# First normalization set by set beside the modulation weights, and the position table as a row part and a column part

## Chip, cores and metric

The kernel runs on one core of a Trainium2 chip. The metric is the device time in microseconds of one execution of the whole program. A profile is one more execution, recorded instruction by instruction; its span runs from the first instruction to the last.

## The reference

One inference step of a network with two layers over 512 latent tokens (a grid of 8 rows and 64 columns) and 128 context tokens, 1024 channels, everything in fp32. Cut to what matters here:

```python
xc, xl = x_prompt, x_sample + grid_pos_embed(512, 1024)   # channels: sin/cos of the row, sin/cos of the column
for l in range(2):
    mod = silu(c) @ w_mod[l] + b_mod[l]                   # for context and for latent tokens: 3 * 1024 values
    shift, scale, gate = split(mod, 3)
    h = rmsnorm(x, norm_g[l]) * (1 + scale) + shift
    z = h @ w_in[l]                                       # inputs of three mixers, their gates, the merge gates
    y_hy = hyena(z...) * silu(gate); y_s5 = s5(z...) * ...; y_gdn = deltanet(z...) * ...
    x = x + gate * (merge(y_hy, y_s5, y_gdn) @ w_out[l])
```

The first half of the position channels (sin and cos of the row) depends on the token's row alone, the second half on its column alone.

## The kernel before

Activations lie transposed: channels on the 128 partitions, in 8 channel tiles (KT = 8), and 640 tokens along each partition. A matrix product in fp32 is made of three matmuls of halves (`mm3`): an operand is split into a rounded part and its remainder (`split`: a cast on ScalarE at L69, a subtraction at L70 on VectorE or, for the gates' weights, on GpSimd). A projection tile is 48 such matmuls (L91), in two weight pieces of 4 channel tiles each; `wr` is a raw weight piece, `wh` and `wl` are its parts, `hh` and `hl` those of the normalized input. Tiles named `pj` are projections of the mixers, tiles named `pg` are gates, which depend on `hh` and `hl` alone and serve as filling work.

`start` does what comes ahead of layer 0: SP loads x (five pieces `xi`), the position table (`pos`) and four sets of modulation weights (`wm`, 2048 KB each); TensorE transposes x channel tile by channel tile (L129), VectorE adds `pos` (L271), ScalarE squares and VectorE sums the squares (L320 to L324), and `rstd_cols` makes 1/rms of each token (`rstd`, L338). `mod_set` multiplies one weight set (L286), copies the result out of PSUM (`mrow`, L289), transposes it and adds the biases (`mod`, L136, L138). Set s gives shift and scale of the channel tiles s and 4 + s alone. `norm_h` spreads `rstd` over the partitions (`dg` L136, two matmuls with ones L352 and L353, copy to `rs` L354) and then normalizes the 8 channel tiles: multiply on VectorE (`xn`), two activations on ScalarE (`hf`, L362), `split` to `hh` and `hl`.

After it the hyena and S5 stage runs, two generators taken in turn, with the gates 0 to 13 as filling work. The S5 tables begin with two powers on GpSimd (`stp` L698 from the step sizes `in_ls`, `smag` L703); the S5 transposes L129 of `M` and products L908 need these tables. The last matmuls of a hyena block are its synthesis (L468 to L473). Then comes the DeltaNet stage with the other gates, then the merge, and the same again for layer 1.

The code is not run in the order in which it is written: a scheduling pass with a timeline of its own places every instruction on its engine's queue, and each queue then runs strictly in that order. A tile in reused memory waits for the tile that it replaces.

Of the kernel before, what the change touches and what calls it, by code (L numbers as in the profile page):

```python
# [12 lines left out]
F32 = mybir.dt.float32  # L13
F32R = mybir.dt.float32r
AF = mybir.ActivationFunctionType
ALU = mybir.AluOpType
# [36 lines left out]
def bc(ap, shape):  # L53
    return ap.to_broadcast(shape)


class Net:
# [98 lines left out]
    def run(self):  # L156
        tc, nc, a = self.tc, self.nc, self.a
        with ExitStack() as es:
# [9 lines left out]
            with self.pool(name="pm0", bufs=4, space=PSUM) as self.pm:  # L168
                self.start()
            for l in range(self.depth):  # L170
                with self.pool(name="pmn", bufs=2, space=PSUM) as self.pm:
                    self.norm_h(l)
# [58 lines left out]
    def start(self):  # L231
# [20 lines left out]
        with self.pool(name="st", bufs=2) as p:  # L252
# [3 lines left out]
            pos = [p.tile([128, KT // 2, NLAT], F32, name="pos%d" % h, bufs=1) for h in range(2)]  # L256
            for h in range(2):
                nc.sync.dma_start(pos[h], a["pos"][4 * h:4 * h + 4].rearrange("k p t -> p k t"))
# [5 lines left out]
            for k in range(KT):  # L264
# [6 lines left out]
                nc.vector.tensor_tensor(xk[:, :NLAT], ps, pos[k // 4][:, k % 4, :], op=ALU.add)  # L271
                nc.scalar.copy(xk[:, NLAT:], pc[:, :128])
                self.square_acc(p, k, xk)
                nc.sync.dma_start(self.xd[0][k], xk)
                self.xs.append(xk)
            for s in range(4):
                self.mod_set(0, s, [wm[s][:, k] for k in range(KT)], self.bank(), self.bank(), p)

# [61 lines left out]
    def norm_h(self, l):  # L340
# [3 lines left out]
        md = self.mod[l]  # L344
        with self.pool(name="nm", bufs=2) as p:
            r = self.rstd
            dg = p.tile([128, 5, 128], F32, name="dg", bufs=1)
            for t in range(5):
                self.ts(nc.vector, dg[:, t, :], self.ident, r[:, t:t + 1])
            rs = p.tile([128, NTOK], F32, name="rs", bufs=1)  # L350
            pa, pb = self.bank(), self.bank()
            nc.tensor.matmul(pa, self.ones, dg[:, 0:4, :], start=True, stop=True)  # L352
            nc.tensor.matmul(pb[:, :128], self.ones, dg[:, 4, :], start=True, stop=True)  # L353
            nc.scalar.copy(rs[:, :NLAT], pa)  # L354
            nc.vector.tensor_copy(rs[:, NLAT:], pb[:, :128])
            for k in range(KT):
                xk = self.xs[k]
                t = p.tile([128, NTOK], F32, name="xn")
# [1190 lines left out]
def _f(x):  # L1549
    return np.ascontiguousarray(x, dtype=np.float32)  # L1550
# [148 lines left out]
```

## Time and profile before

| | before |
|---|---|
| median of 3 runs (lowest to highest) | 3738.56 us (3723.69 to 3741.91) |
| profiled execution | 3732.11 us |
| its span | 3730.3 us |
| mean granted TensorE clock | 0.95 |
| busy: TensorE matmuls / VectorE / ScalarE / GpSimd | 91% / 64% / 38% / 52% |

The busy shares are means over stages with different limits. The profiled execution is one of its own, and times inside it are set against its own time.

### The profile page before, as it was taken

To read this page: it belongs to the slowest core of one execution; us is meant where nothing else is said; L and a number is where in the kernel's file an instruction comes from. 1 tells how busy PE (TensorE), PEld (TensorE's weight loads), DVE (VectorE), ACT (ScalarE), POOL (GpSimd) and SP (SyncE) were. 2 spreads that over 40 slices of the span, in tenths; PEclk is the share of its full clock that TensorE was granted. 3 is DMA by queue.
4 is the path that set the end of the run, shared out by engine and by line. 5 is a ranking of instruction groups with operands and counts; after the bars stand their busy time and mean duration, and the time that the engine had idled before them with its cause. 6 is when DMAs were issued, how large, how long until landed. Compare 5 with 4: busy or idle time off the path is not lost. (4 is left out here: it accounts for less than half of the span.)

```text
span 3730.3 us, 68509 instructions
## 1 busy us (share of the span) xinstructions
PE 3380.0 (91%) x25850; PEld 3220.4 (86%) x25850; DVE 2369.6 (64%) x4615; ACT 1413.4 (38%) x3295; POOL 1942.9 (52%) x2153
## 2 busy tenths in 40 slices
PE   6899898999979898899979999999989898898998
PEld 5798878888979887799978889988889898797998
DVE  6777677777227873743747776677773378875354
ACT  4433232332244445443334333323322545445422
POOL 4777777776345443401336777878763544341010
PEclk7999899999989998999989999999999999899999
DMA  6322334322232212533633222233222322134352
GB/s 242 110 73 82 94 107 115 108 73 63 78 93 65 68 62 68 170 126 109 188 113 98 75 71 83 81 75 81 76 66 77 92 64 78 41 97 139 125 178 89
DMA packets 310602, 363.05 MB, mean 97 GB/s; under 512 B 86814, under 2 KB 190270, under 8 KB 310016
## 3 DMA queue, kind: packets, MB, share of 16 engines
q1 hardware_dynamic: 305368, 358.01, 32.6%
q8 instruction: 204, 3.34, 0.4%
q10 hardware_dynamic: 4904, 0.66, 0.1%
q14 instruction: 126, 1.03, 0.1%
HBM read 291.87 MB, written 66.67 MB: 96 GB/s over the span
## 5 line engine op out<-in xcount | busy, mean ns | idle before, releaser
L91 PE MATMUL pj<-hh,wh 128*128 128x320 f32 x2048 | 666.4, 326 | 60.5 <-ACT wh L69 32.2
L91 PE MATMUL pj<-hh,wl 128*128 128x320 f32 x2048 | 655.5, 322 | 10.5 <-DVE wl L70 8.0
L91 PE MATMUL pj<-hl,wh 128*128 128x320 f32 x2048 | 657.9, 321 | 5.5 <-DVE hl L70 5.4
L70 POOL TENSOR_TENSOR wl<-wr,wh 128x512 fp32r<-128x512 f32 x288 | 392.1, 1365 | 448.9 <-ACT wh L69 388.7
L69 ACT CAST wh<-wr 128x512 fp32r<-128x512 f32 x608 | 374.8, 618 | 659.7 <-PE pj L91 486.3
L91 PEld LDWEIGHTS pj<-hh,wh 128*128 128x128 f32 x2048 | 400.7, 196 | 70.8 <-ACT wh L69 33.6
L91 PE MATMUL pg<-hh,wh 128*128 128x320 f32 x1280 | 415.1, 325 | 15.2 <-ACT wh L69 10.5
L91 PE MATMUL pg<-hh,wl 128*128 128x320 f32 x1280 | 407.6, 323 | 9.3 <-POOL wl L70 9.2
L70 DVE TENSOR_TENSOR wl<-wr,wh 128x512 fp32r<-128x512 f32 x320 | 259.5, 812 | 244.4 <-ACT wh L69 243.1
L91 PEld LDWEIGHTS pj<-hh,wl 128*128 128x128 f32 x2048 | 398.8, 195 | 14.9 <-DVE wl L70 9.3
L91 PE MATMUL pg<-hl,wh 128*128 128x320 f32 x1280 | 411.5, 322 | 0.0
L91 PEld LDWEIGHTS pj<-hl,wh 128*128 128x128 f32 x2048 | 400.3, 195 | 11.1 <-DVE hl L70 8.8
L91 PE MATMUL pj<-yh,wh 128*128 128x320 f32 x1024 | 318.0, 312 | 6.5 <-ACT yh L69 5.1
L91 PE MATMUL pj<-yl,wh 128*128 128x320 f32 x1024 | 318.9, 312 | 2.6 <-DVE yl L70 2.5
L91 PE MATMUL pj<-yh,wl 128*128 128x320 f32 x1024 | 317.5, 311 | 0.0
L91 PEld LDWEIGHTS pg<-hh,wh 128*128 128x128 f32 x1280 | 250.4, 196 | 19.4 <-ACT wh L69 11.6
L91 PEld LDWEIGHTS pg<-hh,wl 128*128 128x128 f32 x1280 | 247.4, 194 | 14.2 <-POOL wl L70 12.5
L91 PEld LDWEIGHTS pg<-hl,wh 128*128 128x128 f32 x1280 | 249.5, 195 | 0.9 <-issue 0.4
L91 PEld LDWEIGHTS pj<-yh,wh 128*128 128x128 f32 x1024 | 193.4, 189 | 8.1 <-ACT yh L69 5.9
L91 PEld LDWEIGHTS pj<-yl,wh 128*128 128x128 f32 x1024 | 193.5, 189 | 4.8 <-DVE yl L70 4.8
L91 PEld LDWEIGHTS pj<-yh,wl 128*128 128x128 f32 x1024 | 193.6, 189 | 0.0
L1514 POOL TENSOR_TENSOR m<-m,gt 128x640 f32<-128x640 f32 x16 | 31.1, 1943 | 295.8 <-DVE gt L132 295.8
(523 smaller groups left out, 8673.3 us busy)
## 6 DMA issues: line engine op xcount, KB each, us to landing
wr<-in_wt SPq DMA_DIRECT2D x608, 256.0 KB, 2.7
gt<-gst SPq DMA_DIRECT2D x160, 160.0 KB, 2.0
gt<-gt SPq DMA_DIRECT2D x64, 320.0 KB, 3.4
wr<-in_wmod SPq DMA_DIRECT2D x64, 256.0 KB, 3.3
Pm<-gcd SPq DMA_DIRECT2D x32, 320.0 KB, 11.0
wm<-in_wmod SPq DMA_DIRECT2D x4, 2048.0 KB, 16.8
M<-ks SPq DMA_DIRECT2D x256, 32.0 KB, 1.8
us<-u SPq DMA_DIRECT2D x16, 328.0 KB, 4.2
```

What stands on the lines that cost most here:

```text
L69: self.nc.scalar.copy(h, src)
L70: (eng or self.nc.vector).tensor_tensor(l, src, h.bitcast(F32), op=ALU.subtract)
L91: ins = self.nc.tensor.matmul(o, w[:, k, :m], x[:, kh * 4 + k, s], start=kh == 0 and k == 0 and i == 0, stop=kh == 1 and k == 3 and i == 2)
L1514: nc.gpsimd.tensor_tensor(m[i], m[i], g, op=ALU.add)
```

## The change

- The position table comes as 8 row values and 64 column values for each channel (128 x 288 numbers in place of two halves of 128 x 4 x 512), is loaded ahead of x, and the add at L271 repeats it along the grid.
- `norm_h` keeps the spreading of `rstd`; the normalization of one channel tile is `norm_k`. In layer 0 both are called in `start`: the spreading ahead of the weight sets, and after set s the tiles s and 4 + s. Layer 1 keeps its order.
- The PSUM pool of `start` has 6 buffers, not 4; the pool of the normalization is open during `start`; the stores of x (`xd`) are written behind the sets.
- Six small loads of the hyena stage (`alt`, `hcw`, `hcb`, `fw1`, `fw2`, `fb`) are issued by SP and no longer by ScalarE.

```diff
-            with self.pool(name="pm0", bufs=4, space=PSUM) as self.pm:
+            with self.pool(name="pm0", bufs=6, space=PSUM) as self.pm:
                 self.start()
             for l in range(self.depth):
-                with self.pool(name="pmn", bufs=2, space=PSUM) as self.pm:
-                    self.norm_h(l)
+                if l:
+                    with self.pool(name="pmn", bufs=2, space=PSUM) as self.pm, self.pool(name="nm", bufs=2) as p:
+                        self.norm_h(l, p)
+                        for k in range(KT):
+                            self.norm_k(l, k, p)
+                self.layer_dram(l)
...
-        with self.pool(name="st", bufs=2) as p:
+        with self.pool(name="nm", bufs=2) as pn, self.pool(name="st", bufs=2) as p:
+            pos = p.tile([128, 288], F32, name="pos", bufs=1)
+            nc.sync.dma_start(pos, a["pos"])
             xi = [p.tile([128, DM], F32, name="xi%d" % t, bufs=1) for t in range(5)]
             for t in range(5):
                 nc.sync.dma_start(xi[t], a["x"][t * 128:(t + 1) * 128])
-            pos = [p.tile([128, KT // 2, NLAT], F32, name="pos%d" % h, bufs=1) for h in range(2)]
-            for h in range(2):
-                nc.sync.dma_start(pos[h], a["pos"][4 * h:4 * h + 4].rearrange("k p t -> p k t"))
+
+            row = pos[:, 0:32].rearrange("p (k r) -> p k r", k=4)
+            col = pos[:, 32:288].rearrange("p (k c) -> p k c", k=4)
...
-                nc.vector.tensor_tensor(xk[:, :NLAT], ps, pos[k // 4][:, k % 4, :], op=ALU.add)
+                sh = [128, 8, 64]
+                g = bc(row[:, k, :].unsqueeze(2), sh) if k < 4 else bc(col[:, k - 4:k - 3, :], sh)
+                nc.vector.tensor_tensor(xk[:, :NLAT].rearrange("p (r c) -> p r c", r=8),
+                                        ps.rearrange("p (r c) -> p r c", r=8), g, op=ALU.add)
                 nc.scalar.copy(xk[:, NLAT:], pc[:, :128])
                 self.square_acc(p, k, xk)
-                nc.sync.dma_start(self.xd[0][k], xk)
                 self.xs.append(xk)
+            self.norm_h(0, pn)
             for s in range(4):
                 self.mod_set(0, s, [wm[s][:, k] for k in range(KT)], self.bank(), self.bank(), p)
+                for k in (s, 4 + s):
+                    self.norm_k(0, k, pn)
+            for k in range(KT):
+                nc.sync.dma_start(self.xd[0][k], self.xs[k])
...
-    def norm_h(self, l):
+    def norm_h(self, l, p):
...
+    def norm_k(self, l, k, p):
+
+        nc, md = self.nc, self.mod[l]
+        xk = self.xs[k]
+        t = p.tile([128, NTOK], F32, name="xn")
+        nc.vector.tensor_tensor(t, xk, self.rs, op=ALU.mult)
+        h = p.tile([128, NTOK], F32, name="hf")
+        for i, (s, e) in enumerate(((0, NLAT), (NLAT, NTOK))):
+            nc.scalar.activation(h[:, s:e], t[:, s:e], AF.Identity, bias=md[:, k, i:i + 1],
+                                 scale=md[:, 8 + k, i:i + 1])
+        self.split(self.hh[:, k, :], self.hl[:, k, :], h)
...
-            nc.scalar.dma_start(self.alt, a["alt"])
+            nc.sync.dma_start(self.alt, a["alt"])
             self.hcw = cp.tile([128, 24, 3], F32, name="hcw")
-            nc.scalar.dma_start(self.hcw, a["hcw"][l].rearrange("p (n c) -> p n c", n=24))
+            nc.sync.dma_start(self.hcw, a["hcw"][l].rearrange("p (n c) -> p n c", n=24))
             self.hcb = cp.tile([128, 24], F32, name="hcb")
-            nc.scalar.dma_start(self.hcb, a["hcb"][l])
+            nc.sync.dma_start(self.hcb, a["hcb"][l])
...
-            nc.scalar.dma_start(w1, a["fw1"][l])
+            nc.sync.dma_start(w1, a["fw1"][l])
             w2 = p.tile([64, 64], F32, name="w2")
-            nc.scalar.dma_start(w2, a["fw2"][l])
+            nc.sync.dma_start(w2, a["fw2"][l])
             fb = p.tile([64, 3], F32, name="fb")
-            nc.scalar.dma_start(fb, a["fb"][l])
+            nc.sync.dma_start(fb, a["fb"][l])
```

Since a scheduling pass sets the order, a few lines move many instructions. On ScalarE, from the weight sets to the first input projection, stood before (`mrow` is a set's copy out of PSUM, `lr`, `li`, `stp` are loads for the S5 tables):

```order
L323 ACTIVATE sqt<-x_219 128x640
L289 COPY mrow<-pb 128x128 x4
L692 DMA lr<-in_lr 128x64
L693 DMA li<-in_li 128x64
L695 DMA stp<-in_ls 64x64 x2
L354 COPY rs<-pb 128x512
L697 DMA s_542<-in_s 128x128
L784 DMA sd<-in_sd 128x16
L362 ACTIVATE hf<-xn,mod_91 128x512
L362 ACTIVATE hf<-xn,mod_91 128x128
L69 CAST wh<-wr 128x512 x2
```

and on the same engine stands now, for the second and third pair of channel tiles (`hh` is the cast that ends a tile's normalization on ScalarE):

```order
L69 CAST hh<-hf 128x640 x2
L302 COPY mrow<-pb 128x128
L377 ACTIVATE hf<-xn,mod_91 128x512
L377 ACTIVATE hf<-xn,mod_91 128x128
L377 ACTIVATE hf<-xn,mod_91 128x512
L377 ACTIVATE hf<-xn,mod_91 128x128
L69 CAST hh<-hf 128x640 x2
L302 COPY mrow<-pb 128x128
```

and behind that, for the fourth pair:

```order
L709 DMA lr<-in_lr 128x64
L710 DMA li<-in_li 128x64
L377 ACTIVATE hf<-xn,mod_91 128x512
L377 ACTIVATE hf<-xn,mod_91 128x128
L377 ACTIVATE hf<-xn,mod_91 128x512
L377 ACTIVATE hf<-xn,mod_91 128x128
L712 DMA stp<-in_ls 64x64 x2
L69 CAST hh<-hf 128x640
L714 DMA s_536<-in_s 128x128
L69 CAST hh<-hf 128x640
L801 DMA sd<-in_sd 128x16
L69 CAST wh<-wr 128x512 x6
```

The loads of `stp` stood ahead of all normalization and stand behind its last activations; the first weight casts (`wh`) stand behind its last cast; each set's copy stands behind the casts of the pair before.

On TensorE, the end of the sets before and their beginning now (`dg` times ones is the spreading of `rstd`, `sqs` the sum of squares):

```order
L129 MATMUL pb<-c_66,mrow 128x128
L286 MATMUL pb<-wm_120,csc 32x128 x32
L129 MATMUL pb<-c_66,mrow 128x128
L352 MATMUL pb<-dg,c_66 128x512
L353 MATMUL pb<-dg,c_66 128x128
L91 MATMUL pj<-hh,wh 128x320
```

and now:

```order
L346 MATMUL pb<-c_66,sqs 128x2 x5
L364 MATMUL pb<-dg,c_66 128x512
L365 MATMUL pb<-dg,c_66 128x128
L299 MATMUL pb<-wm_115,csc 32x128 x32
L129 MATMUL pb<-c_66,mrow 128x128
```

The spreading moved from behind the fourth set to ahead of the first.

On GpSimd, from the end of its constants, before and now (`wl` here are remainders of the gates' weights, `BR` the first product that needs the S5 tables):

```order
L843 MEMSET u 128x8x2
L698 TENSOR_TENSOR stp<-c_66,stp 128x64
L703 TENSOR_TENSOR smag<-c_66,smag 128x64
L70 TENSOR_TENSOR wl<-wr,wh 128x512 x2
L859 TENSOR_TENSOR BR<-lwr,sbr 128x128
```

and now:

```order
L860 MEMSET u 128x8x2
L715 TENSOR_TENSOR stp<-c_66,stp 128x64
L70 TENSOR_TENSOR wl<-wr,wh 128x512 x2
L720 TENSOR_TENSOR smag<-c_66,smag 128x64
L860 MEMSET u 128x8x2
L846 TENSOR_TENSOR E<-E 128x16
L70 TENSOR_TENSOR wl<-wr,wh 128x512 x2
L876 TENSOR_TENSOR BR<-lwr,sbr 128x128
```

Two weight remainders moved ahead of the second power, two more ahead of the first product.

Farther on, the rows of TensorE differ up to about 43% of their number, within the DeltaNet stage of layer 0, and are then the same but for a short stretch in the merge of layer 1. Ahead of the first S5 transposes of `M` stood 156 matmuls of L91 (48 `pj`, 28 `pg`, 48 `pj`, 32 `pg`); now 258. Between those transposes and the next groups stood 24, 12, 24, 23 of them. Ahead of the last synthesis of layer 0 stood 1028 of the layer's 2304 matmuls into `pg`; now 1271. In layer 1 it is 1425 in both.

## Rows read from the trace of the kernel before

**Rows 1.** Windows of the two layers: length, busy us (x instructions) by engine, granted clock, DMA.

```profile
100.00:989.00 889.00, 813.35 (x6322) 759.60 (x6322) 623.54 (x1003) 277.52 (x772) 648.78 (x760) 0.96 0.33 89
989.00:1908.00 919.00, 837.79 (x6489) 812.01 (x6488) 524.98 (x1273) 404.13 (x829) 302.58 (x298) 0.96 0.35 107
1958.00:2854.00 896.00, 835.02 (x6233) 794.81 (x6232) 626.05 (x950) 291.85 (x792) 665.35 (x758) 0.98 0.29 77
2854.00:3712.00 858.00, 792.21 (x6118) 767.31 (x6116) 497.34 (x1174) 379.06 (x777) 251.65 (x261) 0.94 0.32 99
```

**Rows 2.** Windows, the third 10 us, as in Rows 1; last column GB/s.

```profile
20.00:30.00 10.00, 4.45 (x53) 4.15 (x55) 5.27 (x8) 3.11 (x5) 1.73 (x4) 0.65 1.05 387
```

**Rows 3.** DMA view of the first 60 us: issues, KB each, us to landing.

```profile
pos<-in_pos SPq DMA_DIRECT2D x2, 1024.0 KB
```

**Rows 4.** Timeline, DMA issues on SP: start us, us, what.

```profile
24.29 5.20 SPq L487 DMA_DIRECT2D zt<-in_zt  x1
...
42.18 1.07 SPq L81 DMA_DIRECT2D wr<-in_wt  x2
```

**Rows 5.** Timeline, transposes to modulation: start us, us, engine, what [idle before].

```profile
13.99 2.67 DVE L271 TENSOR_TENSOR x<-pb,pos 128x512 f32<-128x512 f32 x4 [9.93 <-DMA pos<-in_pos]
...
20.99 4.53 DVE L324 TENSOR_TENSOR sqs<-sqs,sqt 128x640 f32<-128x640 f32 x5
...
28.21 1.17 POOL L338 TENSOR_TENSOR rstd<-rsv,c 128x5 f32<-128x5 f32 x1 [27.78 <-DVE rsv L138]
...
31.57 0.27 ACT L289 COPY mrow<-pb 128x128 f32<-128x128 f32 x1 [7.13 <-PE pb L286]
...
32.91 0.35 DVE L138 TENSOR_SCALAR mod<-mod,ng 128x2 f32<-128x2 f32 x2
...
40.04 3.58 PE L286 MATMUL pb<-wm,csc 128*32 128x128 f32 x64 [1.88 <-DMA wm<-in_wmod]
```

**Rows 6.** Timeline of VectorE: an add with a repeated operand.

```profile
107.45 0.67 DVE L894 TENSOR_TENSOR M<-T,BR 128x512 f32<-128x512 f32 x1
```

**Rows 7.** Timeline, first normalization and weight casts.

```profile
44.92 0.86 DVE L136 TENSOR_SCALAR dg<-c,rstd 128x128 f32<-128x128 f32 x4
...
47.38 0.58 ACT L354 COPY rs<-pb 128x512 f32<-128x512 f32 x1 [3.40 <-PE pb L353]
...
51.83 1.12 ACT L69 CAST wh<-wr 128x512 fp32r<-128x512 f32 x2
...
55.68 2.29 ACT L362 ACTIVATE hf<-xn,mod 128x512 f32<-128x512 f32 x4 [0.39 <-DVE hl L70]
...
57.87 1.34 ACT L69 CAST hh<-hf 128x640 fp32r<-128x640 f32 x2
```

**Rows 8.** Timeline of TensorE: first input projection, gates, first S5 transposes.

```profile
54.72 0.64 PE L91 MATMUL pj<-hh,wh 128*128 128x320 f32 x1 [7.36 <-ACT hh L69]
...
71.12 0.47 PE L91 MATMUL pj<-hh,wh 128*128 128x320 f32 x1
...
74.31 0.31 PE L91 MATMUL pg<-hh,wh 128*128 128x320 f32 x1
...
78.41 0.31 PE L91 MATMUL pj<-hh,wh 128*128 128x320 f32 x1
...
93.06 0.66 PE L129 MATMUL pb<-c,M 128*128 128x128 f32 x4 [0.80 <-DVE M L896]
...
116.11 0.39 PE L91 MATMUL pj<-hh,wl 128*128 128x320 f32 x1
```

**Rows 9.** Timeline, S5 step loads and GpSimd.

```profile
45.27 1.99 ACTq L695 DMA_DIRECT2D stp<-in_ls  x2
...
49.40 10.55 POOL L698 TENSOR_TENSOR stp<-c,stp 128x64 f32<-128x64 f32 x1 [17.09 <-DMA stp<-in_ls]
60.51 10.55 POOL L703 TENSOR_TENSOR smag<-c,smag 128x64 f32<-128x64 f32 x1 [0.56 <-DVE smag L701]
71.02 2.52 POOL L70 TENSOR_TENSOR wl<-wr,wh 128x512 fp32r<-128x512 f32 x2
```

More of the change, by code (lines that the diff above doesn't have):

```diff
@@ L343, in norm_h @@
         self.hl = self.hp.tile([128, KT, NTOK], F32R, name="hl", tag="hl")
[L344 to L358, printed above, removed]
-                nc.vector.tensor_tensor(t, xk, rs, op=ALU.mult)
-                h = p.tile([128, NTOK], F32, name="hf")
-                for i, (s, e) in enumerate(((0, NLAT), (NLAT, NTOK))):
-                    nc.scalar.activation(h[:, s:e], t[:, s:e], AF.Identity, bias=md[:, k, i:i + 1],
-                                         scale=md[:, 8 + k, i:i + 1])
-                self.split(self.hh[:, k, :], self.hl[:, k, :], h)
@@ new lines, in norm_h @@
+        r = self.rstd
+        dg = p.tile([128, 5, 128], F32, name="dg", bufs=1)
+        for t in range(5):
+            self.ts(nc.vector, dg[:, t, :], self.ident, r[:, t:t + 1])
+        self.rs = p.tile([128, NTOK], F32, name="rs", bufs=1)
+        pa, pb = self.bank(), self.bank()
+        nc.tensor.matmul(pa, self.ones, dg[:, 0:4, :], start=True, stop=True)
+        nc.tensor.matmul(pb[:, :128], self.ones, dg[:, 4, :], start=True, stop=True)
+        nc.scalar.copy(self.rs[:, :NLAT], pa)
@@ new lines, in norm_h @@
+        nc.vector.tensor_copy(self.rs[:, NLAT:], pb[:, :128])
+    def norm_k(self, l, k, p):
[8 more added lines that the diff above has]
+        self.split(self.hh[:, k, :], self.hl[:, k, :], h)
@@ L365, in norm_h, with layer_dram @@
+    def layer_dram(self, l):
         self.md = self.dp.tile([KT, 128, NTOK], F32, name="md%d" % l)
@@ L1569, in shape_constants @@
     pos = np.concatenate([np.sin(er), np.cos(er), np.sin(ec), np.cos(ec)], -1)
-    out["pos"] = _f(pos.T.reshape(KT, 128, NLAT))
+    pos = pos.T.reshape(KT, 128, NLAT)
+    out["pos"] = _f(np.concatenate([pos[0:4, :, ::64].transpose(1, 0, 2).reshape(128, -1),
+                                    pos[4:8, :, :64].transpose(1, 0, 2).reshape(128, -1)], 1))
     t = np.arange(256)[:, None] * 1.0
```

## The prediction, made before the changed kernel ran

> **What bounds the kernel now.** I read the page first (TensorE is the fullest engine and does the same work in both programs), then the windows of the stages, then the timeline of the first 120 us, engine by engine. In the windows the reader is to see that layer 0 and layer 1 spend their time alike and that TensorE is idle for little of it: 889 - 813.4 = 75.6 us and 919 - 837.8 = 81.2 us in layer 0, 61.0 and 65.8 us in layer 1 [rows 1]. No other engine is near that. So the kernel is TensorE's work plus its waits, and a lead that TensorE gains at the start is kept as far as later waits don't grow. In the timeline the start is a chain: position table and x in, transposes, squares, rstd, four sets of modulation weights, then the normalization of eight channel tiles on ScalarE and VectorE with TensorE trickling behind it; the first input projection begins at 54.72 and gives way to the gates only at 74.31 [rows 8].
>
> **The change part by part.**
>
> *Position table.* Two loads of 1024 KB go [rows 3]; 128 x 288 fp32 (144 KB) come. The 1904 KB less at 387 GB/s [rows 2] bring the weight sets in 5.0 us earlier. TensorE waits for a set only once, 1.88 us for the fourth [rows 5], so this alone is worth about 2 us. The first add waited for the table until 13.99 [rows 5]; now the transposes set its time. The five squares summed last, 4.53 us [rows 5], stay, so I take their end from 25.52 to 23.8 (bounds 25.5 and 22.5). The add with a repeated operand is not in the trace in this form: eight adds at 2.67 / 4 = 0.67 us [rows 5], and a VectorE operation with a repeated operand and as many elements takes 0.67 us too [rows 6], so no cost.
>
> *Rstd row ahead of the sets.* From the end of the squares to rstd it takes 29.38 - 25.52 = 3.86 us [rows 5], so rstd stands at 27.7. From the first diagonal tile to the end of the row's copy: 47.96 - 44.92 = 3.0 us [rows 7], so the row is there at 30.8. This step is now ahead of the first set on TensorE, which before started during rstd: set 0 runs 30.3 + 3.58 [rows 5] = 33.9. From a set's copy out of PSUM to its modulation columns: 33.26 - 31.57 = 1.7 us [rows 5], so the first pair of channel tiles can start at 35.6.
>
> *Pairs.* ScalarE needs 2.29 us for a pair's four activations and 1.34 us for two casts [rows 7], 3.63 us. It also copies the next set out of PSUM, and in the new order that copy stands behind casts, so ScalarE then waits the 1.7 us until the modulation is back. A pair thus costs 5.3 us, not 3.6, and the last cast ends at 35.6 + 3 x 5.3 + 3.6 = 55.1. If the columns came in time it would be 50.9 (four pairs and three copies of 0.27). So the normalization is not hidden behind loads that end at 35: half of it comes after.
>
> *First projection.* All weight casts stand behind the last pair on ScalarE; one cast is 0.56 us [rows 7] and the rest on VectorE takes about as long, so the first matmul comes at 56.3, later than 54.72 before. But it no longer waits for channel tiles. Its 48 matmuls have a pitch of (74.31 - 71.12) / 12 = 0.266 us, at a granted clock near half, or (78.41 - 74.31) / 28 = 0.146 us, at the full one [rows 8]: 7.0 to 12.8 us, I take 9.7, since TensorE comes out of a long idle stretch. It ends at 66.0 where it ended at 74.31: 8.3 us gained (bounds 5 and 15).
>
> *What is late next: GpSimd.* The loads of the S5 step are issued by ScalarE; they stood ahead of the normalization and now stand behind the last activations, at 35.6 + 16 + 2.3 = 53.9. From that issue to GpSimd's power it takes 49.40 - 45.27 = 4.1 us [rows 9], so it runs 58.0 to 68.5 instead of 49.40 to 59.95. Queued behind it are the remainders of the gates' weights: the first is there 2.52 / 2 = 1.3 us later [rows 9], at 69.8, and the gates' fifth matmul waits some 3 us for it. The lead shrinks to 5 us there. The second power is now behind these two remainders and ends at 68.5 + 2.5 + 10.55 = 81.6 instead of 71.06. So the S5 tables, and the S5 transposes that came at 93.06 [rows 8], are ready only at about 103.6. The new order answers with gates: 258 projection matmuls stand ahead of these transposes instead of 156. From 69.8 TensorE has 206 of them left, 206 x 0.146 = 30 us, some 2 us of the filter's matmuls, and perhaps 4 us of waits for GpSimd, and arrives at 106. The kernel before has its 240th at 116.11 [rows 8] and its 258th 18 x 0.146 later, at 118.7. The 12.7 us between, less about 4.5 us of S5 work that it had done by then (an estimate: three groups of transposes like the one at 93.06 and two of products), leave **8 us** of lead (bounds 3 and 12).
>
> *Six small loads move from ScalarE's queue to SP's.* Three of them land behind the load of zt, whose issue slot took 5.20 us, since the queue was backed up; the first weights were issued at 42.18 [rows 4]. If each of the three took as long, the first weights would be issued at 42.2 - 5.0 + 15.6 = 52.8 and the first matmul would come 1 to 2 us later; if they take what an unhindered issue does, below half a microsecond, nothing happens, since the weights are needed only at 55. I take nothing. The Trainium skill ("DMA: Bandwidth & Descriptors", Issuing engines are not separate DMA queues) says that loads of all issuing engines interleave on the same 16 DMA engines, and that spreading the issuing saves sequencer time alone; by it moving them changes the landing of nothing, and the sum would be the same 8 us.
>
> *The rest of layer 0.* The order differs through about the first 43% of TensorE's rows and is then the same. The one shift that matters: at the last hyena synthesis 1271 of the layer's 2304 gate matmuls are done instead of 1028, so 243 x 0.146 = 35 us of filling work move out of the DeltaNet stage into the hyena stage. Layer 1, with 1425 by that point in both programs, shows what such a spread gives: it idles 61.0 + 65.8 = 126.8 us where layer 0 idles 156.8 [rows 1], 30 us less. In proportion, 243 / 397 x 30 = 18 us. Layer 0 has another load (the next layer's modulation) and its moved gates need GpSimd, which is busy for 649 of 889 us [rows 1]; so I take a quarter, 4 us (bounds: 18 gained, 10 lost). The Trainium skill ("Trainium Kernel Development and Optimization", Best Practices) wants TensorE judged by its weight loads, not by matmul busy time: by that column the layers idle 236.4 and 191.9 us [rows 1], 44 us apart, and the same proportion would give 27 us instead of 18. That would make the gaining rival below larger; what the trace cannot say is which of the two columns the moved gates fill.
>
> *Sum.* 8 + 4 = 12 us off. The profiled execution took 3732.1 us, 1.8 us over its span and 6.4 us below the median of the three runs; the four together have a mean of 3734. I take 3734 - 12 = **3722 us**, 0.44% below the median.
>
> **The rivals.**
>
> *The idle time of layer 0 becomes that of layer 1.* For it: the same code, the same share of gates. Against it: the modulation loads. It gives 8 + 18 = 26 us, 3708 us.
>
> *The lead is lost to the S5 chain.* GpSimd's power starts 8.6 us later, and the S5 transposes 11 to 14 us later. If the hyena and S5 stage is paced by that chain and not by TensorE, the stage ends up to 11 us later and gates merely fill. For it: from the first S5 product to the last synthesis the stage takes 889 us in layer 0 and 896 us in layer 1, though the gates in it differ by 397 matmuls. Against it: TensorE is busy for 813 of the 889 us [rows 1]. Its time is 3734 to 3745, no change by the bound below.
>
> *Slower: the 243 gates displace instead of filling.* Each gate needs two weight remainders on GpSimd, 1.3 us each [rows 9], in a stage where GpSimd is 73% busy. If all 35 us lengthen the hyena stage, and the DeltaNet stage is held by VectorE's chain and doesn't shrink, the kernel is 35 - 8 = 27 us slower, 3761 us; it turns to slower by the bound from 27 of the 35 us on. Against it: TensorE was idle for 81 us in the second stage [rows 1], too little for a chain that would not shrink.
>
> **How the numbers follow.** A measurement of this kernel can tell about 0.5% (19 us) from no change. My forecast has 0.42; between -4 and -20 us about it, a quarter of that falls beyond 19 us. The idle time of layer 1 has 0.28, nearly all of it faster; the lost lead 0.20, no change; the displaced gates 0.10, slower with the most of it. Faster: 0.25 x 0.42 + 0.27 = 0.38; slower 0.09; no change 0.53. The range reaches from 3699 (18 us of filling and 12 us of lead are 30, and the spread of a median of 6) to 3747, a little past the lost lead; the displaced gates and half of the largest gains lie outside. My forecast's own range is 3714 to 3732.
>
> **What would show it.** Right: the first projection matmul at 55 to 58, the gates at 64 to 68, then a wait of 2 to 5 us for a weight remainder of GpSimd; the power at 56 to 60; ScalarE idle for 1 to 2 us between pairs; no wait for the weight sets; the S5 transposes at 102 to 108; the last synthesis between 975 and 990. Wrong: pairs 3.7 us apart and the first projection done before 60 (more gain), S5 transposes waiting for VectorE (the chain paces), a hyena stage that ends after 1000 with a DeltaNet stage as long as before.

## The result, and the profile after

The changed kernel takes 3698.55 us (median of 4 runs, 3684.26 to 3700.27) where the kernel before took 3737.82 us beside it (4 runs): a ratio of 0.9893, 95% interval 0.9857 to 0.9929. A second comparison gave 3694.36 us (6 runs) against 3730.01 us: 0.9916 (0.9898 to 0.9935). So the change gains 31 to 40 us. The forecast was 12 to 16 and its range ended at 3699: the sign was right, the size was not. By the prediction's own bound of 19 us this is "faster", to which it gave a chance of 0.38.

The start went as forecast. This is the timeline of the first 104 us after (start us, us, engine, what [idle before]); it answers to [rows 5, 7 to 9]:

```profile
19.74 4.53 DVE L337 TENSOR_TENSOR sqs<-sqs,sqt 128x640 f32<-128x640 f32 x5
...
26.90 1.17 POOL L351 TENSOR_TENSOR rstd<-rsv,c 128x5 f32<-128x5 f32 x1 [26.47 <-DVE rsv L138]
...
31.39 0.58 ACT L366 COPY rs<-pb 128x512 f32<-128x512 f32 x1 [8.21 <-PE pb L364]
...
35.81 2.29 ACT L377 ACTIVATE hf<-xn,mod 128x512 f32<-128x512 f32 x4 [1.19 <-DVE mod L138]
...
41.17 2.29 ACT L377 ACTIVATE hf<-xn,mod 128x512 f32<-128x512 f32 x4 [1.67 <-DVE mod L138]
...
56.23 10.69 POOL L715 TENSOR_TENSOR stp<-c,stp 128x64 f32<-128x64 f32 x1 [21.14 <-DMA stp<-in_ls]
...
56.86 0.64 PE L91 MATMUL pj<-hh,wh 128*128 128x320 f32 x1 [6.11 <-ACT wh L69]
...
67.50 0.31 PE L91 MATMUL pg<-hh,wh 128*128 128x320 f32 x1
...
68.23 0.42 PE L91 MATMUL pg<-hh,wl 128*128 128x320 f32 x1
...
103.83 0.60 PE L129 MATMUL pb<-c,M 128*128 128x128 f32 x4
```

The squares end at 24.27, the second and the third pair follow 5.36 us behind the one ahead with ScalarE waiting for `mod` in between (the fourth 6.2 us), the first projection gives way to the gates at 67.50, and the first S5 transposes come at 103.83.

What was not forecast shows in the windows of the two layers, whose columns are those of [rows 1] and whose four windows answer to its four:

```profile
108.00:999.00 891.00, 823.45 (x6434) 768.38 (x6432) 621.68 (x994) 279.19 (x781) 650.41 (x767) 0.96 0.32 90
999.00:1874.00 875.00, 801.81 (x6276) 777.61 (x6274) 518.00 (x1274) 392.60 (x811) 289.60 (x289) 0.96 0.34 109
1922.00:2814.00 892.00, 830.21 (x6237) 790.50 (x6236) 626.71 (x950) 291.90 (x791) 665.42 (x758) 0.98 0.29 78
2814.00:3664.00 850.00, 784.68 (x6120) 757.67 (x6118) 501.94 (x1175) 379.00 (x777) 253.35 (x261) 0.96 0.32 100
```

The hyena stage of layer 0 takes 112 more TensorE instructions than in [rows 1] and 2 us more time; the DeltaNet stage behind it (with the merge) takes 213 fewer and 44 us less. Layer 1 came out 12 us shorter too. Its rows stand in nearly the same order in both, and in the profiles below, which have as many matmuls of each kind done at its last synthesis, it took 1797.6 to 1807.3 us in every kernel but the one before, whose single profile shows 1810.6 with a mean granted clock of 0.95 (0.97 in the second profile after, at 1799.2 us, for as many TensorE instructions). I count that difference as variation between executions, which a single profile can't show, and read the change in layer 0.

That the gain is in layer 0, and how it is made up, is seen best beside the second profile of the changed kernel (3693.80 us, near its median). Windows of the start, the hyena stage, and the stages behind it until layer 1 begins (the matmul that spreads its `rstd`), first of the kernel before:

```profile
0.00:100.00 100.00, 63.76 (x503) 54.30 (x504) 62.70 (x175) 38.75 (x81) 45.09 (x43) 0.80 0.72 249
100.00:988.70 888.70, 813.05 (x6319) 759.30 (x6319) 623.25 (x1002) 277.52 (x772) 648.78 (x760) 0.96 0.33 88
988.70:1919.70 931.00, 840.45 (x6506) 814.22 (x6505) 531.37 (x1283) 405.03 (x832) 312.41 (x313) 0.95 0.34 107
sum 1919.70, PE 1717.26 PEld 1627.83 DVE 1217.32 ACT 721.30 POOL 1006.29; mean PE 572.42 PEld 542.61 DVE 405.77 ACT 240.43 POOL 335.43
```

and of the changed kernel's second profile:

```profile
0.00:108.80 108.80, 73.19 (x608) 64.59 (x609) 68.27 (x182) 45.93 (x90) 51.56 (x44) 0.86 0.67 231
108.80:1006.40 897.60, 826.38 (x6435) 770.25 (x6434) 620.99 (x994) 278.57 (x781) 651.35 (x768) 0.96 0.32 90
1006.40:1892.80 886.40, 804.91 (x6286) 779.56 (x6285) 523.32 (x1283) 393.98 (x814) 299.29 (x304) 0.95 0.34 107
sum 1892.80, PE 1704.48 PEld 1614.40 DVE 1212.59 ACT 718.47 POOL 1002.20; mean PE 568.16 PEld 538.13 DVE 404.19 ACT 239.49 POOL 334.07
```

Layer 1 begins 26.9 us earlier (35.1 in the first profile after). For the same 13,324 instructions of TensorE (one that crosses a window's edge counts in both), TensorE is busy for 12.8 us less (1717.3 to 1704.5) and idle for 14.1 us less (202.4 to 188.3). The start itself ends 8.8 us later, but with 105 more matmuls done, about 15 us at 0.146: a lead of some 7 us, as forecast. The other 20 (28 in the first profile) arise behind it. The experiments ask why.

### The profile page after: what moved, and what is told of

It reads as the page before. It is cut to its first block, busy times and chain, and to the rows that moved or that the text cites. A ratio compares the mean times of both kernels' runs of the same rounds, so it can differ in the third digit from the quotient of the medians.

```text
span 3682.2 us, 68543 instructions
## 1 busy us (share of the span) xinstructions
PE 3350.0 (91%) x25850; PEld 3190.0 (87%) x25850; DVE 2370.8 (64%) x4615; ACT 1410.5 (38%) x3294; POOL 1940.5 (53%) x2153
## 5 line engine op out<-in xcount | busy, mean ns | idle before, releaser
L91 PE MATMUL pj<-hh,wh 128*128 128x320 f32 x2048 | 664.2, 325 | 59.3 <-ACT wh L69 31.2
L91 PE MATMUL pj<-hl,wh 128*128 128x320 f32 x2048 | 656.7, 321 | 4.2 <-DVE hl L70 4.1
L91 PE MATMUL pj<-hh,wl 128*128 128x320 f32 x2048 | 652.9, 320 | 2.1 <-POOL wl L70 1.4
L91 PEld LDWEIGHTS pj<-hh,wh 128*128 128x128 f32 x2048 | 398.8, 195 | 69.0 <-ACT wh L69 32.8
L91 PE MATMUL pg<-hh,wh 128*128 128x320 f32 x1280 | 411.6, 322 | 13.2 <-ACT gst L1441 8.5
L91 PE MATMUL pg<-hh,wl 128*128 128x320 f32 x1280 | 402.8, 319 | 10.9 <-POOL wl L70 10.8
L91 PE MATMUL pg<-hl,wh 128*128 128x320 f32 x1280 | 406.6, 318 | 0.0
L91 PEld LDWEIGHTS pj<-hl,wh 128*128 128x128 f32 x2048 | 398.8, 195 | 8.8 <-DVE hl L70 6.2
L91 PEld LDWEIGHTS pj<-hh,wl 128*128 128x128 f32 x2048 | 396.8, 194 | 5.5 <-POOL wl L70 2.7
L91 PE MATMUL pj<-yh,wh 128*128 128x320 f32 x1024 | 317.2, 311 | 5.1 <-ACT yh L69 3.5
L91 PE MATMUL pj<-yl,wh 128*128 128x320 f32 x1024 | 318.5, 312 | 3.0 <-DVE yl L70 2.8
L91 PE MATMUL pj<-yh,wl 128*128 128x320 f32 x1024 | 317.1, 310 | 0.0
L91 PEld LDWEIGHTS pg<-hh,wh 128*128 128x128 f32 x1280 | 246.5, 193 | 18.4 <-ACT gst L1441 11.2
L91 PEld LDWEIGHTS pg<-hh,wl 128*128 128x128 f32 x1280 | 244.3, 192 | 16.2 <-POOL wl L70 15.3
L91 PEld LDWEIGHTS pg<-hl,wh 128*128 128x128 f32 x1280 | 246.3, 192 | 0.9 <-issue 0.5
L91 PEld LDWEIGHTS pj<-yh,wh 128*128 128x128 f32 x1024 | 192.4, 188 | 7.5 <-ACT yh L69 5.2
L91 PEld LDWEIGHTS pj<-yl,wh 128*128 128x128 f32 x1024 | 192.9, 188 | 5.2 <-DVE yl L70 5.1
L91 PEld LDWEIGHTS pj<-yh,wl 128*128 128x128 f32 x1024 | 192.9, 189 | 0.0
```

The source lines that it names most:

```text
L91: ins = self.nc.tensor.matmul(o, w[:, k, :m], x[:, kh * 4 + k, s], start=kh == 0 and k == 0 and i == 0, stop=kh == 1 and k == 3 and i == 2)
```

## The experiments

Each run is a kernel of its own. All ratios are to the kernel before on the same chip. Stages are read from one profile each, as above: the start ends with the first product of the S5 part (with its tile `U`), the hyena stage with the last matmul of layer 0's last synthesis. In the two profiles after, the hyena stage differs by 6 us and the DeltaNet stage with the merge by 1; in two pairs of kernels with the same gate counts at every synthesis they differ by 4 and 2 (six loads alone and 6 PSUM buffers) and by 8 and 9 (before and the first S5 run). A few us of one stage therefore say nothing here. "Gates early" counts matmuls into `pg` that stand in TensorE's order ahead of the last matmul of that last synthesis; before has 1051. The prediction and most texts below give 1028 for before, its count ahead of that synthesis' first matmul, but count the other kernels as here, so that those differences are 23 off (after has 1271 by both counts).

| kernel | ratio, 95% interval | first U product, us | hyena stage | DeltaNet and merge | layer 1 begins | gates early |
|---|---|---|---|---|---|---|
| before | 1 | 100.0 | 888.7 | 931.0 | 1919.7 | 1051 |
| after (again) | 0.9916, 0.9898 to 0.9935 | 108.8 | 897.6 | 886.4 | 1892.8 | 1271 |
| table alone | 1.0021, 1.0008 to 1.0034 | 94.4 | 905.4 | 933.9 | 1933.7 | 1003 |
| normalization alone | 1.0018, 1.0006 to 1.0030 | 113.8 | 913.2 | 904.0 | 1931.0 | 1225 |
| six loads alone | 0.9965, 0.9953 to 0.9977 | 97.2 | 919.4 | 894.6 | 1911.2 | 1184 |
| after without the six loads | 0.9968, 0.9954 to 0.9982 | 111.4 | 878.2 | 923.1 | 1912.7 | 1040 |
| before, 6 PSUM buffers | 0.9961, 0.9947 to 0.9975 | 96.7 | 915.0 | 896.7 | 1908.4 | 1184 |
| after, gates held at the end | 1.0013, 1.0002 to 1.0024 | 108.1 | 897.4 | 926.3 | 1931.8 | 1056 |
| before, 19 gates first | 0.9944, 0.9926 to 0.9962 | 100.1 | 897.0 | 911.3 | 1908.4 | 1044 |
| after, S5 step early, `mrow` on VectorE | 0.9964, 0.9950 to 0.9979 | 89.3 | 897.0 | 922.1 | 1908.4 | 1051 |
| after, S5 step early | 0.9944, 0.9925 to 0.9964 | 95.5 | 891.0 | 916.5 | 1903.0 | 1082 |
| before, modulation late | 0.9955, 0.9940 to 0.9970 | 100.6 | 913.2 | 897.5 | 1911.3 | 1471 |
| after, modulation late | 0.9954, 0.9937 to 0.9971 | 108.7 | 884.6 | 913.4 | 1906.7 | 1488 |
| after, gates held behind synthesis 5 | 1.0025, 1.0013 to 1.0038 | 108.8 | 910.5 | 914.0 | 1933.3 | 1070 |
| after, 12 gates first | 0.9939, 0.9921 to 0.9957 | 108.0 | 894.6 | 896.4 | 1899.0 | 1214 |
| after, 8 gates first | 0.9949, 0.9929 to 0.9969 | 108.9 | 894.9 | 885.0 | 1888.8 | 1212 |

**The change in parts.** The table's hunks alone, on before; the normalization's hunks alone (whole table, six loads on ScalarE); the six loads alone:

```diff
-            nc.scalar.dma_start(self.alt, a["alt"])
+            nc.sync.dma_start(self.alt, a["alt"])
...
-            nc.scalar.dma_start(fb, a["fb"][l])
+            nc.sync.dma_start(fb, a["fb"][l])
```

and the same six lines taken back in after.

Table alone: 

> The kernel before with the position table's edit alone: the row part and the column part in one small load, the first additions read a repeated operand, the start otherwise as before. The order that comes out has 1003 gate matmuls ahead of layer 0's last hyena synthesis (before 1028, after 1271). Theory G (the gain that was not forecast comes from gate matmuls that moved from layer 0's DeltaNet stage into its hyena stage, some 27 us for 243 of them, 0.11 us each): the start gains under 1 us, 25 gates fewer cost 3, so 3737 to 3742. Rival S (all of the gain comes from the earlier start): the loads end earlier and nothing waits for them long, 3735 to 3738. Both within 0.5% of before.

Normalization alone: 

> The kernel after without the table's edit (the whole table is loaded as before) and with the six small loads issued by ScalarE as before: the normalization of layer 0 between the sets of modulation weights alone. 1225 gate matmuls stand ahead of layer 0's last hyena synthesis (before 1028, after 1271). Theory G: 8 us of the start and 197 gates at 0.11 us, 3738 - 8 - 22 = 3708 (3703 to 3715). Rival S: the start is what gains, so nearly all of it, 3699 to 3703. Rival M (the six loads moved from ScalarE's queue to SP's are what gains): 3726 to 3738.

Six loads alone: 

> The kernel before with only the six small loads of the filter and the hyena stage issued by SP in place of ScalarE; the start is that of before. 1184 gate matmuls stand ahead of layer 0's last hyena synthesis (before 1028). Theory G: 156 gates at 0.11 us, 3738 - 17 = 3721 (3715 to 3728), with layer 0's DeltaNet stage shorter by some 20 us and the start unchanged. Rival S: no earlier start, so 3734 to 3741. Rival M: 3710 to 3715.

After without them: 

> The kernel after with the six small loads issued by ScalarE as before; the start keeps all of the change (split table, two channel tiles behind each set). 1040 gate matmuls stand ahead of layer 0's last hyena synthesis (before 1028, after 1271). Theory G: 8 us of the start, nothing else, 3738 - 8 - 1 = 3729 (3724 to 3734). Rival S: the start is what gains, 3697 to 3702. Rival M: 3711 to 3729.

The table alone came out 8 us slower (its text allowed 4), the normalization alone 7 us slower where none of the three theories allowed a loss, the loads alone 13 us faster. The parts don't add up: their sum is a loss of 2 us, and the whole gains 31 to 40. Rival S wanted 35 us and more from both kernels that keep the normalization between the sets; they end 7 us above and 12 us below before. They begin like after (rstd row spread at 31.0 and 29.3, after 29.3; first gate at 68.3 and 67.5, after 67.5), but their S5 transposes come at 109.7 and 107.5 instead of 103.8, so a part of the lead is missing; runs below with after's whole start settle S. Theory G in its plain form, a price for each early gate, fell with the normalization alone too: it has 1225 early gates and its DeltaNet stage is 27 us shorter, as G says, but its hyena stage gives that back. Part of it can be named. In the waits of TensorE there (us, times, longest) stand

```profile
PE pg L295 <- DMA wr<-in_wmod: 18.8, 14, 5.5
PE pb L129 <- DVE M L909: 9.3, 6, 3.3
```

of which after shows the first as 6.9 us (9.2 in its second profile) and the second as 3.2 (3.3). Why the modulation's weights come late in that order stays open.

**Does the start, a load, or the order decide?** After once more; before with one number changed:

```diff
-            with self.pool(name="pm0", bufs=4, space=PSUM) as self.pm:
+            with self.pool(name="pm0", bufs=6, space=PSUM) as self.pm:
```

After with layer 0's later gates kept behind the last synthesis:

```diff
-                            self.gates(l, NG1, NX[l])
+                            if l == 0:
+                                self.gates(l, NG1, 22)
+                                with tc.issue_after(self.syn.ins):
+                                    self.gates(l, 22, NX[l])
```

and before with five more gates offered to the hyena stage:

```diff
-                        self.gates(l, 0, NG1)
+                        self.gates(l, 0, NG1 + 5 * (l == 0))
```

After again: 

> The kernel after once more, timed on one chip beside the three others and the kernel before. Both theories: 0.986 to 0.993 of before. A profiled run that isn't the lowest of its set should end layer 0's DeltaNet stage some 35 us ahead of before again, if the gain sits there.

Six PSUM buffers: 

> The kernel before with six PSUM buffers in place of four in the start, nothing else: the start and the six loads are those of before, and the order that comes out is nearly that of the run with the six loads moved (1184 gate matmuls ahead of layer 0's last hyena synthesis, at the same places). Theory O (what each edit is worth beyond the start is the order of layer 0's hyena stage that happens to come out): as the run with the moved loads, 0.994 to 0.998 of before. Rival M (SP's issues of the six loads were worth that run's 0.35%): 0.999 to 1.002.

Gates held at the end: 

> The kernel after, with layer 0's gates from number 22 on held behind the last hyena synthesis: the start and the order up to the seventh synthesis are those of after, and 1056 gate matmuls in place of 1271 stand ahead of the last one (215 matmuls, 31 us of TensorE at 0.146). Theory G (the gates that moved fill idle time of the hyena stage): that stage gets shorter by under 15 us and the DeltaNet stage longer by 31 to 40, so 15 to 25 us are lost: 0.994 to 0.997 of before. Rival O (the two stages trade matmuls one for one and the gain is in how the hyena stage's own steps follow each other): the hyena stage gets shorter by 25 to 35 us and the time stays within 8 us of after's.

Nineteen gates first: 

> The kernel before with five more gates of layer 0 (240 matmuls) offered to the hyena stage ahead of the modulation's second part; 1044 gate matmuls stand ahead of the last synthesis (before 1028), more of them early in the stage (912 by the fourth synthesis, before 672), and the modulation's matmuls later. The start is that of before. Theory O: the order alone moves the time, by up to 15 us either way, 0.995 to 1.004, and where it goes is read from the idle time of TensorE in layer 0's hyena stage (before 75.7 us). Rival S (only the start matters): 0.999 to 1.001.

The six buffers give what the six loads gave (0.9961 and 0.9965), with nearly the same order and no load moved: rival M fell, and moving the loads is worth nothing by itself that these intervals (about 5 us either way) show. The Trainium skill ("DMA: Bandwidth & Descriptors", Issuing engines are not separate DMA queues) says that DMAs run on the same 16 engines whichever engine started them, so that only time for issuing is saved; these two runs agree. Holding 215 gates takes the whole gain away: 1.0013 where theory G had 0.994 to 0.997 and rival O less than 8 us of loss: rival O fell, and G said too little. Rival S fell too: the start is after's, with the first U product at 108.1. The windows of its last two iterations of the hyena stage, from synthesis to synthesis, and of the stages behind it:

```profile
825.90:935.20 109.30, 96.10 (x711) 88.97 (x710) 78.81 (x119) 28.89 (x81) 82.29 (x87) 0.94 0.23 61
935.20:1005.50 70.30, 55.65 (x406) 52.76 (x405) 33.37 (x67) 14.14 (x35) 25.69 (x30) 0.88 0.24 53
1005.50:1931.80 926.30, 833.84 (x6501) 809.15 (x6499) 534.60 (x1283) 401.69 (x829) 310.06 (x312) 0.96 0.33 107
```

and of the same two iterations of after:

```profile
827.80:939.10 111.30, 104.58 (x816) 99.13 (x815) 79.65 (x123) 34.98 (x94) 87.95 (x91) 1.00 0.27 76
939.10:1006.40 67.30, 66.80 (x516) 64.89 (x516) 32.94 (x63) 15.75 (x38) 33.14 (x35) 1.00 0.32 81
```

The iterations take 179.6 us with 1117 matmuls and 178.6 us with 1332. The 215 gates were free there, and the DeltaNet stage pays 39.9 us for them. Nineteen gates first gained 21 us with before's start and before's number of early gates; the order alone moves this kernel by more than half of what the change gains.

**An earlier start with before's order.** The S5 step sizes are loaded first of all, into a tile of their own, and layer 0's `mrow` copies go to VectorE; in a second run the step sizes alone:

```diff
+        self.s5e = mp.tile([128, 64], F32, name="stp0")
+        for d in range(2):
+            nc.scalar.dma_start(self.s5e[64 * d:64 * d + 64, :], bc(a["ls"][0, d:d + 1, :], [64, 64]))
...
-        nc.scalar.copy(rows, ps[:, 0:128])
+        (nc.vector.tensor_copy if l == 0 and s < 4 else nc.scalar.copy)(rows, ps[:, 0:128])
```

And the modulation's second part (`mod_rest`) offered behind gates 14 to 38, on before and on after:

```diff
-        if i0 == 0:
-            self.mod_rest(l, p)
...
                             self.gates(l, NG1, NX[l])
+                            self.mod_rest(l, self.gp[0])
```

Step sizes and copies: 

> The kernel after with two edits to the start: the step of the S5 tables is loaded ahead of all else, so GpSimd's first long power runs during the loads, and layer 0's four copies of the modulation's row go to VectorE in place of ScalarE. From the hyena stage's first synthesis on its TensorE order counts the same matmuls at each synthesis as that of the kernel before (1051 gate matmuls by the last one, after 1271), so this is a start that is earlier than after's with before's order. Theory G (what after gained beyond 8 us is the gates that are reached sooner): only the start's lead is left, first U product at 90 to 95 (before 100.0, after 107.8 with 72 more gates done), 0.996 to 0.999 of before. Rival S (the start's lead is what gains): at least after's, 0.992 or less.

Step sizes alone: 

> The kernel after with the S5 step loaded ahead of all else alone: first U product at 88 to 96 with 67 gates done in place of 156, 1082 gate matmuls by the last synthesis. Theory G: the start's lead and 54 gates at 0.15 us: 0.994 to 0.998. Rival S: 0.992 or less.

Modulation late, on before: 

> The kernel before with the modulation's second part (512 small matmuls and their loads) offered behind layer 0's gates 14 to 38 in place of behind gate 13, so that it runs in the DeltaNet stage: the start is before's, and 1471 gate matmuls stand ahead of the last hyena synthesis (before 1028, after 1271). Theory G: the hyena stage takes 443 more of them for under 25 us, and the DeltaNet stage loses 65 us of gates and takes on the modulation, whose iterations in the hyena stage held 5 to 10 us more idle time each: 0.985 to 0.995. Rival S (only the start matters): 0.999 to 1.001. Rival X (the modulation's loads cost the DeltaNet stage what the gates leave): 0.997 to 1.003.

Modulation late, on after: 

> The kernel after with the same edit, the modulation's second part behind gates 14 to 38: 1488 gate matmuls by the last synthesis (after 1271). Theory G: after's 0.9916 and a part of what the edit gives before, less for each gate, since the hyena stage's idle time in after is 71 us and was 76: 0.984 to 0.990. Rival X: 0.991 to 0.997.

The first of them shows a start apart from the order. GpSimd's timeline there has the first power at 16.64, during the loads, and the second at 50.91 (before 60.51):

```profile
16.64 10.56 POOL L718 TENSOR_TENSOR stp<-c,stp 128x64 f32<-128x64 f32 x1 [16.21 <-DMA stp<-in_ls]
50.91 11.45 POOL L723 TENSOR_TENSOR smag<-c,smag 128x64 f32<-128x64 f32 x1 [14.31 <-issue]
```

Windows of its start, its hyena stage and the stages behind it:

```profile
0.00:89.30 89.30, 56.06 (x504) 49.32 (x505) 62.14 (x179) 38.24 (x77) 45.52 (x42) 0.87 0.73 254
89.30:986.30 897.00, 814.24 (x6318) 760.37 (x6317) 626.06 (x1002) 278.45 (x772) 652.11 (x761) 0.96 0.31 88
986.30:1908.40 922.10, 831.10 (x6506) 806.74 (x6505) 532.45 (x1283) 403.11 (x830) 312.65 (x313) 0.96 0.34 108
```

With before's order behind it, a first U product 10.7 us earlier makes layer 1 begin 11.3 us earlier and the kernel 13 us faster (0.9964): over both stages a lead of the start is kept one for one, as the prediction held, and nothing comes on top. Stage by stage it is not seen: the hyena stage took 8 us longer than before's, the other 9 us less, and the last synthesis came only 2.4 us earlier. The step sizes alone came out inside theory G's bounds too. The modulation late gained 17 us on before, a little less than theory G's least and more than the rivals had; on after it lost 14 us against after itself, which fits rival X and not theory G. More early gates are thus no gain where the 512 small matmuls of the modulation take their place in the DeltaNet stage: on after that stage got 27 us longer though 217 gates had left it, and TensorE waited 15.0 us there for the modulation's weights.

**Which gates.** After with layer 0's gates from 14 on held behind the fifth synthesis, where before has them; and the modulation offered behind gate 11 and behind gate 7:

```diff
+                                with tc.issue_after(self.syn[4].ins):
+                                    self.gates(l, NG1, NX[l])
...
-                        self.gates(l, 0, NG1)
+                        self.gates(l, 0, 12 if l == 0 else NG1)
```

Held behind synthesis 5: 

> The kernel after with layer 0's gates from number 14 on held behind the fifth hyena synthesis, where they begin in the kernel before: after's start and after's modulation (by the fifth synthesis 672 gate matmuls, before 672, after 862), 1070 by the last one (before 1051, after 1271). Theory G (190 gates that reach the fifth iteration are what after gained beyond its start): the DeltaNet stage gets 201 gates back at 0.163 us each, the slope of that stage's length over the gates left for it in twelve profiles, +33, and the hyena stage gives up to 15 back, so 0.996 to 1.000 of before, with only the start's lead left. Rival O (the gain is in how after's order runs apart from where the gates stand): within 8 us of after, 0.990 to 0.994.

Twelve gates first: 

> The kernel after with the modulation's second part offered behind gate 11 of layer 0 in place of gate 13: the start is after's, 1214 gate matmuls by the last synthesis (after 1271). By the slopes over twelve profiles (0.163 us of the DeltaNet stage for a gate left to it, 0.075 us of the hyena stage for one placed there): 57 gates, 5 us more than after, 0.990 to 0.996 of before. Rival O: anywhere from 0.986 to 1.002.

Eight gates first: 

> The kernel after with the modulation's second part offered behind gate 7 of layer 0: the start is after's, the modulation stands in the second and third iterations of the hyena stage, 1212 gate matmuls by the last synthesis. By the same slopes 5 us more than after, 0.990 to 0.996 of before. Rival O: anywhere from 0.986 to 1.002.

The held gates cost 41 us against after (1.0025 to 0.9916), slightly more than theory G said; the other two came out inside its 0.990 to 0.996, which rival O's bounds allowed as well. The windows of iterations 3 to 6 of the hyena stage and of the stages behind it, after:

```profile
375.60:496.50 120.90, 102.66 (x877) 89.52 (x875) 80.57 (x146) 32.24 (x98) 77.38 (x99) 0.89 0.41 114
496.50:613.10 116.60, 102.47 (x886) 90.70 (x885) 87.29 (x154) 33.77 (x105) 86.75 (x112) 0.93 0.43 120
613.10:726.40 113.30, 105.61 (x788) 99.46 (x787) 79.12 (x120) 34.80 (x101) 87.02 (x105) 0.92 0.30 89
726.40:827.80 101.40, 97.75 (x747) 93.38 (x747) 75.07 (x117) 32.69 (x87) 69.23 (x81) 0.98 0.26 72
```

and with the gates held behind the fifth synthesis:

```profile
375.50:496.90 121.40, 102.91 (x877) 90.32 (x875) 80.88 (x146) 32.25 (x98) 76.92 (x99) 0.89 0.39 114
496.90:613.80 116.90, 103.75 (x885) 92.11 (x884) 87.13 (x154) 33.77 (x105) 86.68 (x112) 0.91 0.43 120
613.80:732.60 118.80, 91.19 (x627) 82.82 (x627) 79.74 (x122) 29.97 (x91) 82.61 (x101) 0.81 0.22 62
732.60:833.20 100.60, 96.02 (x740) 92.48 (x739) 72.64 (x118) 32.55 (x85) 65.35 (x77) 0.98 0.28 71
1019.30:1933.30 914.00, 831.54 (x6488) 806.88 (x6486) 528.41 (x1283) 402.74 (x831) 308.99 (x313) 0.96 0.34 108
```

Up to the fourth synthesis the two run alike. The fifth iteration has 161 matmuls fewer and takes 5.5 us more: TensorE is idle for 27.6 us there instead of 7.7, and its granted clock is 0.81 instead of 0.92. (In the first profile after, this iteration takes 113.3 us too.) The stages behind pay 27.6 us for the 201 gates. The last two iterations take 7.5 us more as well, with 245 gates in place of 264; that stays unexplained, and what the holding costs apart from the gates' place was not separated.

Before has the modulation in that iteration. It is seen by the lines of its small matmuls (duration ns, first and last start), before and after (second profile):

```profile
L286 PE MATMUL pg<-wr,csc x512: 272/273/423, 406.5 to 725.3; 128*32 128x128 f32 x171
```

```profile
L299 PE MATMUL pg<-wr,csc x512: 272/273/423, 381.8 to 635.9; 128*32 128x128 f32 x171
```

They end 89 us earlier after, at the head of iteration 5 and no longer in iteration 6, and gates 14 and up, which stand behind them, have one more iteration to fill.

## Why the prediction missed

*What bounds the kernel*: right in the main. The time is TensorE's work plus its waits, and a lead of the start is kept (the S5 step run, 10.7 in and 11.3 out). But it took the work as the same in both programs, and the same instructions were busy for 12.8 us less in layer 0.

*Position table*: right in the trace. The squares end at 24.27 (forecast 23.8), there is no wait for a weight set, and an add with the repeated operand takes 0.63 to 0.69 us (forecast 0.67).

*Rstd row and pairs*: right. Set 0 from 31.71, pairs from 35.81 (35.6) at 5.36 us (5.3), the fourth at 6.2, ScalarE waiting 1.7 to 2.5 us between them; the first projection at 56.86 (56.3) and done at 67.50 (66.0): 6.8 us gained where 8.3 stood.

*GpSimd*: the power at 56.23 (58.0). The fifth gate matmul, forecast to wait some 3 us for the first remainder, came 0.29 us after the one ahead of it: the power was 1.8 us early and the first projection 1.5 us late. That wait was wrong, and it cost little. The S5 transposes came at 103.83 (106, window 102 to 108).

*Lead of the start*: 8 us forecast. By the prediction's own accounting 118.7 - 103.83 - 4.5 gives 10.4; by the first U product 7. Right within its bounds of 3 and 12.

*Six loads*: right, no cost or gain of their own shows.

*The rest of layer 0, 4 us*: this is the term that failed. The prediction named the mechanism, gates that fill idle time of the hyena stage, worked out 18 us from layer 1, and then took a quarter for fear of the modulation loads and GpSimd. Measured, it is 26.9 - 7 = 20 us in one profile and 28 in the other, above its bound of 18. Neither took the gain away in this order: in the last two iterations gates cost nothing, in the fifth less than nothing. (In the normalization alone the waits for the modulation's weights did cost some 10 us.) And idle time was only half of it, 14.1 of 26.9 us; the proportion was made of idle time alone, while TensorE's busy time fell by another 12.8 for the same work. Its other proportion, 27 us by the weight loads, meets the first profile, but that column does not hold the whole gain either: in the windows above its idle time fell by 13.5 us and its busy time by 13.4.

A part of the 12.8 goes with the granted clock. The trace's clock records put TensorE at the lower of its two levels (1.2 and 2.4 GHz) for 204 us of layer 0 before and for 186 in the second profile after. By the prediction's pitches, 0.266 and 0.146 us for a matmul, 18 us less of it is worth at most 8 us (an estimate). Over all seventeen profiles the busy time of layer 0 follows the time at the lower level (correlation 0.89), and before's single profile lies 8 us above that line; what the rest is stays open.

*Its signal for "wrong"* needed two things, a hyena stage that ends after 1000 and a DeltaNet stage as long as before. The first half came (1006.4; 998.9 in the first profile), the second did not. Its signal for "right", a last synthesis between 975 and 990, failed: the stage began later and grew by 2 to 9 us. The two rivals without a gain are refuted in their outcome. The S5 chain's had one half right: the last synthesis came 10 to 18 us later (it said up to 11) while gates filled; but the DeltaNet stage with the merge then gave back 45 us, which its "no change" left out. That this chain paces the stage is not borne out: in the S5 step run the first U product came 10.7 us earlier, the last synthesis 2.4. And the gates did not displace: for 112 to 116 TensorE instructions more the hyena stage grew by 2 to 9 us, and the next one shrank. The rival "idle time of layer 0 becomes that of layer 1" (3708) had mechanism and sign, and was still 10 to 14 us short.

What stays open: why the scheduling pass gave this order its early modulation. That is not a property of the change's parts, since the normalization alone and after without the six loads, whose starts are after's up to the first gates, came out 38 and 19 us above after. So the 20 us and more beyond the lead belong to the order that came out and not to the edits: as far as the change goes, they are luck. And no run beat after. The early S5 step together with after's place of the gates was not tried, since every order with that start put fewer gates early.

## What to carry to other kernels

Where a scheduling pass orders the program, an edit to the start is worth its own lead, here one for one, plus whatever the new order does elsewhere, and that second part (20 to 28 us gained here; from 21 gained to 8 lost in runs that changed little else) can be the larger; count in the new order where the filling work lands, stage by stage, before costing the edit. Filling work can cost nothing in one place (the last two hyena iterations here) and its full time in another (the DeltaNet stage), though TensorE is busy for about nine tenths of both stages, so price each place apart: by straight lines through twelve profiles (all but those with the modulation late and those of the last experiment) a gate matmul left for the DeltaNet stage and merge costs 0.163 us, one placed in the hyena stage 0.075, the second line with a wide scatter (correlations 0.93 and 0.57). To tell an edit's own worth from the order's, change the order without the edit, and hold the suspected instructions where they stood.

## What the runs showed of the hardware

More idle time came with slower matmuls. In the fifth iteration above TensorE had 161 matmuls fewer and 19.9 us more idle time, and the mean granted clock of the stretch, between its two levels of 1.2 and 2.4 GHz, was 0.81 instead of 0.92: 627 matmuls were busy for 91.2 us (145 ns each) where 788 were for 105.6 (134 ns). Over layer 0 the same 13,324 instructions were busy for 1699 to 1724 us in the seventeen profiles, and the granted clock stood at the lower level for 173 to 247 us of it.

A power on GpSimd with 128 x 64 elements took 10.5 to 11.5 us in all seventeen profiles (layer 0's two), and 10.56 during the loads of the start as well.

GpSimd held VectorE up in one kind of work and not in another. In the first profile after, two products of 128 x 64 on VectorE (L718, L719) took 1.30 and 1.32 us beside GpSimd's subtractions for the weights (66.89 to 69.42). During a power, from 60.51 to 71.06 before, products of that size took 0.21 to 0.23 us.
